# Every second low part of the weights in the first block made by GpSimd instead of VectorE

## The chip, the core and the metric

The kernel runs on one NeuronCore of a Trainium2 chip. The metric is the device time of one execution in microseconds (us), from the first to the last instruction and what lies around it. The engines are named as in the profile: PE is TensorE's matrix multiplication (PEld its weight loads), DVE is VectorE, ACT is ScalarE, POOL is GpSimd, SP the engine from which the DMAs are issued.

## What is computed

Two blocks of two layers each on 256 tokens of width 1024, all in float32. The first block is the one that the change touches: each layer is a norm, one wide input projection, a gated delta rule with 4 heads, a latent attention with 8 heads, a linear recurrence of width 512, and an output projection with a residual sum. The second block (feed-forward layers, another recurrence, two more attentions) follows it.

```python
def hybrid_layer(x, cos, sin, norm_gain, w_in, ...):
    h = rmsnorm(x, norm_gain)
    proj = h @ w_in
    (gq, gk, gv, gb, ga, gz, mq, mkv, mkr, mz, lx, lz) = jnp.split(proj, offsets, axis=-1)
    ...
    o_a = gated_delta_rule(q, k, v, g, beta)
    ...
    o_b = causal_block_attention(...).astype(dt) * jax.nn.silu(mz)
    ...
    o_c = rg_lru(u, ...).astype(dt) * jax.nn.silu(lz)
    mixed = jnp.concatenate([o_a, o_b, o_c], axis=-1)
    return x + mixed @ w_out
```

## The kernel before

Activations lie transposed, as tiles of 128 features by 256 tokens. Weights come from memory in chunks of 1 MB (`raw`, 2048 columns, 3 buffers), and every product of float32 numbers is made of three products of a shorter type (fp32r): each operand is split into a high part, which is the operand rounded to that type, and a low part, which is what the rounding left over. For the weights `wsplit` (line 680) does that: ScalarE copies the weights into `wh`, which rounds them, and VectorE subtracts `wh` from `raw` and writes `wl`. Parts of over 384 columns have buffers of their own, 3 for `wh` and 3 for `wl`, of up to 1024 columns; smaller ones lie in a pool of other tiles. A split of 1024 columns serves one unit of PE work: 8 tiles of weights, with three products each (`unit`, through `mm3`), or two, one of them twice as wide (`unit_wide`). In each unit the product with the low part of the first tile stands among the first three, so PE needs `wl` soon after `wh`.

`hybrid` (line 1314) writes down one layer of the first block: the scalars of the delta rule, the projections for the delta rule (`gdn_proj`), the latent attention (`mla_q`, `mla_kv`, `mla_pair`), the recurrence (`lru_pair`), gates, and the output projection over 16 chunks' halves (`unit_wide` and `feed`, which adds the result into `x` and prepares the next stage). The projections go through `proj`, which calls `wsplit` for 128 output features at a time. Per layer `wsplit` is called 67 times: 57 with 1024 columns, 4 with 768, 4 with 384 and 2 with 288.

None of this is the order in which the engines work. Every instruction is first noted (`Order.note`), with its dependences, and `schedule` (line 430) then plans the order of all engines together, with a duration for each from `cost` (line 378), the buffers in `SLOTS`, and a priority by place in the program. It then issues the instructions in the planned order; on the chip each engine works through its own list in order. For GpSimd `cost` books 147 + 2.11 ns for each column (line 411), for a VectorE subtraction 68 + 1.042 ns. `trace` (line 1758) writes down the whole program and calls `hybrid` for layers 0 and 1 at lines 1775 and 1799.

GpSimd has work of its own in the first block: masks, sums of squares, rope products, and powers (`pow`, on a few columns). All loads are issued by SP.

Of the kernel before, what the change touches and what calls it, by code (L numbers as in the profile page):

```python
# [9 lines left out]
F32 = mybir.dt.float32  # L10
# [3 lines left out]
ALU = mybir.AluOpType  # L14
# [275 lines left out]
class Tracer:  # L290


    def __init__(self, order, eng):
        self.order, self.eng = order, eng
# [252 lines left out]
class Kern:  # L547
    def __init__(self, ctx, tc, aps):
        self.tc, self.aps = tc, aps
        nc = self.nc = Order(tc.nc)  # L550
        self.n = 0
        self.const = ctx.enter_context(tc.tile_pool(name="const", bufs=1))
        self.pool = ctx.enter_context(tc.tile_pool(name="work", bufs=1))
        self.ps = ctx.enter_context(tc.tile_pool(name="ps", bufs=1, space=PSUM))
        self.x = self.fixed([P, 8, S], "x")
        self.prm = self.fixed([P, NPRM], "prm")
        self.cst = self.fixed([P, NCST], "cst")
        self.ident = self.c("ident")
        self.ones = self.c("ones")
        self.tri_ones = self.const.tile([P, S], F32R, tag="tri_ones", name="tri_ones")  # L560
        self.ones_r = self.tri_ones[:, P:S]
        self.mhalf = self.fixed([P, 1], "mhalf")
        self.phalf = self.fixed([P, 1], "phalf")
        self.tiny = self.fixed([P, 1], "tiny")
        nc.vector.memset(self.mhalf, -0.5)
        nc.vector.memset(self.phalf, 0.5)
        nc.vector.memset(self.tiny, 1e-34)
        self.off = {}

        self.dram = ctx.enter_context(tc.tile_pool(name="dram", bufs=1, space=DRAM))  # L570
        n = 64 * 2064
        self.tri_in = self.dram.tile([n], F32, tag="tri_in", name="tri_in")
        self.tri_out = [self.dram.tile([n], F32, tag=f"tri_out{g}", name=f"tri_out{g}") for g in range(2)]
        self.rows = self.dram.tile([12, 3, P], F32, tag="rows", name="rows")
# [105 lines left out]
    def wsplit(self, src):  # L680
        nc = self.nc
        shape = (P, src.shape[1], src.shape[2])
        n = shape[1] * shape[2]
        h = self.tile("wh" if n > 384 else "s3", shape, F32R)
        l = self.tile("wl" if n > 384 else "s3", shape, F32R)
        nc.scalar.activation(h, src, AF.Copy)
        nc.vector.tensor_tensor(l, src, h.bitcast(F32), ALU.subtract)
        return h, l

    def mm3(self, out, a, b, start, stop):  # L690
# [1058 lines left out]
def build(tc, aps, out, stop=None):  # L1749
    with ExitStack() as ctx:  # L1750
        K = Kern(ctx, tc, aps)
        trace(K, out, stop)
        K.nc.schedule()
        with tc.manual_schedule():
            K.nc.issue()


def trace(K, out, stop):
    nc, V = K.nc, K.nc.vector

    def done(tag):
        if stop == tag:
            nc.sync.dma_start(out.rearrange("p (k t) -> p k t", k=8), K.x)
            return True
        return False

    def stage(gain, fin=K.fin_x, **kw):
        st = K.new_stage(gain, **kw)
        st["fin"] = fin
        return st  # L1770
    raw = K.start()
    st = stage(K.p("norm_gain0"))
    K.first_stage(st)
    nxt = stage(K.p("norm_gain1"))
    K.hybrid(0, st, [nxt], raw)
    if done("h0"):
        return


    fg = K.fixed([P, 8], "fg")  # L1780
    V.tensor_tensor(fg, K.p("fin"), K.p("f1n0"), ALU.mult)

    def fin2(st):
        v1, ms2 = K.meansq(st["sq"]), K.meansq(st["sq2"])
        r1, v2, r2, r12 = [K.col(2) for _ in range(4)]
        K.pow(r1, v1, -0.5)
        V.tensor_scalar(v2, ms2, -1e-6, None, ALU.add)
        V.tensor_tensor(v2, v2, r1, ALU.mult)
        V.tensor_tensor(v2, v2, r1, ALU.mult)
        V.tensor_scalar(v2, v2, 1e-6, None, ALU.add)  # L1790
        K.pow(r2, v2, -0.5)
        V.tensor_tensor(r12, r2, r1, ALU.mult)
        st["rb"] = K.bcast(r12)
        r1b = K.bcast(r1)
        for k in range(8):
            V.scalar_tensor_tensor(K.x[:, k, :], K.x[:, k, :], K.p("fin", k, 1), r1b, ALU.mult, ALU.mult)
    st = nxt
    nxt = stage(fg, fin2, sq_gain=K.p("fin"))
    K.hybrid(1, st, [nxt], [K.chunk("win1", 4, 72) for _ in range(2)])
    if done("fin"):  # L1800
        return
    K.memory()
    st, nxt = nxt, stage(K.p("mix0"))
    K.ffn(st, "gu10", "dn10", [nxt])
    if done("f10"):
        return
    st, nxt = nxt, stage(K.p("f2n0"))
    K.hgrn(st, [nxt])
    if done("m0"):
        return  # L1810
    st, nxt = nxt, stage(K.p("f1n1"))
    K.ffn(st, "gu20", "dn20", [nxt])
    K.shared_kv(nxt)
    st, nxt = nxt, stage(K.p("mix1"))
    K.ffn(st, "gu11", "dn11", [nxt])
    if done("f11"):
        return
    st, nxt = nxt, stage(K.p("f2n1"))
    K.fox(st, [nxt])
    if done("m1"):  # L1820
        return
    K.ffn(nxt, "gu21", "dn21", [])
    ov = out.rearrange("p (k t) -> p k t", k=8)
    for j in range(8):
        nc.sync.dma_start(ov[:, j, :], K.x[:, j, :])
# [16 lines left out]
```

## Time and profile before

| | us |
|---|---|
| median of 3 runs | 1556.71 |
| lowest and highest | 1555.79, 1559.02 |
| the profiled execution | 1554.0 |
| its span, first to last instruction | 1552.2 |

The first block takes the first 490 us or so of the span (the feed-forward weights of the second block are first loaded at 506 us). In the rows below, a row of instructions shows the engine, the operation, the tiles as out<-in and their shapes; `s` and `col` are general tiles in SBUF, `acc` and `mix` are in PSUM, `x` is the residual, `cst` and `prm` are constants and parameters, all in SBUF. All lines are L543, the line that issues the planned order, so groups are told apart by their tiles.

### The profile page before, as it was taken

What the parts mean: (1) busy time and instruction counts of PE and PEld (TensorE: products, weight loads), DVE (VectorE), ACT (ScalarE), POOL (GpSimd) and SP (SyncE); (2) the same over time, 40 slices, a digit from 0 to 9 for tenths busy, and PEclk for the clock granted to TensorE, in tenths of its full rate; (3) what the DMA queues carried; (4) which work ended last, traced back from release to release, by engine and by line L of the source; (5) the groups of instructions that cost most, each with busy time, mean ns of one, the idle gap of its engine ahead of it and who ended that gap; (6) DMA issues with size and microseconds to landing.
All of it is one profiled execution on the core that took longest, in us unless ns stands there. A gap on an engine that the chain in (4) does not pass through costs nothing.

```text
span 1552.2 us, 27102 instructions
## 1 busy us (share of the span) xinstructions
PE 1528.0 (98%) x10216; PEld 1383.8 (89%) x10216; DVE 1209.6 (78%) x2459; ACT 892.8 (58%) x1689; POOL 324.8 (21%) x372
## 2 busy tenths in 40 slices
PE   8999999999999999999999999999999999999998
PEld 8989999998988988889997888889888889888887
DVE  8998979996998777667889777665777677877764
ACT  5458755457776666546455555555665567555542
POOL 2300002310214222202112222121222321132210
PEclk9999999999999999999999999999999999999999
DMA  8343545342545555553334555554555743355553
GB/s 285 121 121 135 167 148 186 118 150 110 166 149 178 178 190 190 190 191 128 129 137 136 190 190 176 188 180 163 191 190 181 258 138 110 136 172 184 181 188 118
DMA packets 54587, 257.58 MB, mean 166 GB/s; under 512 B 11308, under 2 KB 21688, under 8 KB 27576
## 3 DMA queue, kind: packets, MB, share of 16 engines
q1 hardware_dynamic: 54456, 255.85, 48.6%
q8 instruction: 81, 1.33, 0.4%
q14 instruction: 50, 0.41, 0.1%
HBM read 252.39 MB, written 3.43 MB: 165 GB/s over the span
## 4 chain that ended last, share of the span: by engine, by line
PE 83%; DVE 10%; issue 2%; ACT 2%; POOL 2%; DMA 1%; SPq 0%; POOLq 0%; DVEq 0%
PE acc L543 73%; PE mix L543 10%; DVE s L543 6%; DVE wl L543 2%; POOL col L543 2%; ACT s L543 1%; DVE x L543 1%; DVE col L543 1%; ACT wh L543 1%; DMA s<-tri_in 0%; POOL s L543 0%; DMA x<-in_x_dram 0%; ACT L543 0%; SPq L543 0%; POOLq L543 0%
## 5 line engine op out<-in xcount | busy, mean ns | idle before, releaser
L543 PE MATMUL acc<-s,wh 128*128 128x512 f32 (+1 forms) x4224 | 1216.9, 353 | 3.8 <-DVE x L543 2.8
L543 PE MATMUL acc<-s,wl 128*128 128x256 f32 x3360 | 951.3, 283 | 0.1
L543 PEld LDWEIGHTS acc<-s,wh 128*128 128x128 f32 x4224 | 743.3, 190 | 116.2 <-DVE s L543 2.9
L543 ACT ACTIVATE wh<-raw 128x1024 fp32r<-128x1024 f32 (+1 forms) x470 | 489.4, 1041 | 492.5 <-PE acc L543 397.0
L543 DVE TENSOR_TENSOR wl<-raw,wh 128x1024 fp32r<-128x1024 f32 (+1 forms) x470 | 569.2, 1212 | 199.7 <-ACT wh L543 195.3
L543 PEld LDWEIGHTS acc<-s,wl 128*128 128x128 f32 x3360 | 638.5, 190 | 2.0 <-DVE wl L543 0.7
L543 POOL TENSOR_TENSOR s<-s,s 128x256 f32<-128x256 f32 x251 | 220.7, 880 | 712.2 <-DVE s L543 360.7
L543 DVE TENSOR_TENSOR s<-s,s 128x256 fp32r<-128x256 f32 (+6 forms) x302 | 131.5, 446 | 36.7 <-POOL s L543 30.4
L543 PE MATMUL mix<-s,s 128*128 128x128 f32 (+5 forms) x1072 | 150.6, 280 | 5.1 <-DVE s L543 1.9
L543 ACT ACTIVATE s<-s 128x256 fp32r<-128x256 f32 (+3 forms) x311 | 135.6, 445 | 21.3 <-DVE s L543 17.7
L543 PEld LDWEIGHTS mix<-s,s 128*128 128x128 f32 (+4 forms) x1072 | 119.3, 166 | 22.8 <-DVE s L543 4.3
L543 PE MATMUL acc<-wh,s 128*128 128x256 f32 x640 | 125.5, 288 | 0.1
L543 DVE TENSOR_TENSOR s<-acc,s 128x256 f32<-128x256 f32 (+2 forms) x222 | 104.5, 471 | 10.8 <-PE acc L543 9.6
L543 PEld LDWEIGHTS acc<-wh,s 128*128 128x128 f32 x640 | 102.6, 191 | 0.9 <-ACT s L543 0.5
L543 ACT ACTIVATE s<-acc 128x256 f32<-128x256 f32 (+2 forms) x231 | 88.7, 387 | 24.5 <-PE acc L543 24.1
L543 DVE SCALAR_TENSOR_TENSOR x<-acc,x 128x256 f32<-128x256 f32 x192 | 78.3, 420 | 25.9 <-PE acc L543 23.4
L543 POOL TENSOR_TENSOR col<-col,mhalf 128x2 f32<-128x2 f32 (+2 forms) x31 | 47.0, 1519 | 220.8 <-DVE col L543 188.2
L543 PE MATMUL acc<-wl,s 128*128 128x256 f32 x320 | 91.8, 287 | 0.0
L543 ACT ACTIVATE s<-mix 128x128 f32<-128x128 f32 (+6 forms) x208 | 65.3, 328 | 43.6 <-PE mix L543 41.0
L543 DVE SCALAR_TENSOR_TENSOR s<-s,s 128x256 f32<-128x256 f32 (+2 forms) x168 | 82.4, 495 | 2.0 <-ACT s L543 1.7
L543 POOL TENSOR_TENSOR s<-s,cst 128x256 f32<-128x256 f32 x36 | 35.3, 991 | 160.3 <-DVE s L543 120.2
L543 PEld LDWEIGHTS acc<-wl,s 128*128 128x128 f32 x320 | 61.2, 191 | 0.2
(96 smaller groups left out, 772.3 us busy)
## 6 DMA issues: line engine op xcount, KB each, us to landing
raw<-in_gu_dram SPq DMA_DIRECT2D x88, 1024.0 KB, 4.9
raw<-in_win_dram SPq DMA_DIRECT2D x36, 1024.0 KB, 4.9
raw<-in_dn_dram SPq DMA_DIRECT2D x32, 1024.0 KB, 4.9
raw<-in_wo_dram SPq DMA_DIRECT2D x24, 1024.0 KB, 4.9
raw<-in_wina_dram SPq DMA_DIRECT2D x13, 1024.0 KB, 4.9
raw<-in_dn_dram SPq DMA_DIRECT2D x16, 768.0 KB, 4.2
raw<-in_winb_dram SPq DMA_DIRECT2D x7, 1024.0 KB, 4.8
raw<-in_wkv_dram SPq DMA_DIRECT2D x6, 1024.0 KB, 4.9
```

What stands on the lines that cost most here:

```text
L543: getattr(getattr(self.nc, op.eng), op.fn)(*op.args, **op.kw)
```

## The change

A counter runs over all calls of `wsplit`. Where `share` is 2, which is set for the two calls of `hybrid` alone, and a split has more than 384 columns, the subtraction of every second call (even count) is noted for GpSimd instead of VectorE. Instruction, operands and buffers stay the same. The planner sees the other engine and its cost and plans anew.

```diff
@@ -566,6 +566,7 @@
         self.off = {}
+        self.nsplit, self.share = 0, 0
@@ -684,7 +685,9 @@
         nc.scalar.activation(h, src, AF.Copy)
-        nc.vector.tensor_tensor(l, src, h.bitcast(F32), ALU.subtract)
+        self.nsplit += 1
+        eng = nc.gpsimd if n > 384 and self.share and self.nsplit % self.share == 0 else nc.vector
+        eng.tensor_tensor(l, src, h.bitcast(F32), ALU.subtract)
         return h, l
@@ -1772,7 +1775,9 @@
+    K.share = 2
     K.hybrid(0, st, [nxt], raw)
+    K.share = 0
@@ -1796,7 +1801,9 @@
+    K.share = 2
     K.hybrid(1, st, [nxt], [K.chunk("win1", 4, 72) for _ in range(2)])
+    K.share = 0
```

## Rows read from the trace of the kernel before

**Rows 1.** The page: span, and busy time, share and instructions of two engines.

```profile
span 1552.2 us, 27102 instructions
PE 1528.0 (98%) x10216; PEld 1383.8 (89%) x10216; DVE 1209.6 (78%) x2459; ACT 892.8 (58%) x1689; POOL 324.8 (21%) x372
```

**Rows 2.** Busy time by stretch: stretch, its length, then each engine's us (instructions).

```profile
35.00:91.00 56.00, 54.30 (x421) 52.02 (x420) 55.22 (x149) 26.62 (x44) 15.98 (x15) 1.00 0.41 140
...
258.00:336.00 78.00, 76.63 (x601) 74.04 (x601) 75.02 (x208) 37.51 (x65) 20.30 (x18) 1.00 0.40 137
...
410.00:456.00 46.00, 44.96 (x347) 43.13 (x346) 45.74 (x101) 37.67 (x82) 12.38 (x11) 1.00 0.53 174
...
0.00:490.00 490.00, 479.53 (x3637) 447.21 (x3638) 435.02 (x1050) 300.82 (x625) 84.21 (x99) 0.99 0.47 157
```

**Rows 3.** Chain of waits, shares by line: 35-91, 258-336, 410-456, 185-258, 120-164 us.

```profile
by line: DVE s L543 58.4%; DVE wl L543 17.2%; PE acc L543 8.6%; PE mix L543 5.9%; issue 4.8%; POOL col L543 2.9%; DVE col L543 2.4%
...
by line: DVE s L543 37.7%; PE acc L543 30.1%; DVE wl L543 11.7%; DMA s<-tri_in 8.3%; PE mix L543 4.0%; POOL col L543 3.1%; issue 2.3%; DVE col L543 2.3%; SPq L543 0.5%; DVEq L543 0.1%
...
by line: PE acc L543 34.7%; DVE s L543 21.8%; PE mix L543 17.5%; DVE wl L543 14.6%; issue 5.9%; ACT s L543 3.1%; ACT L543 2.4%; ACT wh L543 2.1%
...
by line: PE acc L543 52.6%; PE mix L543 12.5%; issue 11.5%; DVE s L543 11.0%; DVE x L543 4.7%; DVE wl L543 3.1%; POOL s L543 2.6%; ACT wh L543 1.5%; ACT s L543 1.1%; POOLq L543 0.0%
...
by line: PE acc L543 61.2%; PE mix L543 39.1%
```

**Rows 4.** Low parts (tile wl) on DVE: all to 490 us, then three stretches.

```profile
L543 DVE TENSOR_TENSOR wl<-raw,wh x122: 944/1219/1753, 13.3 to 489.4; 128x1024 fp32r<-128x1024 f32 x114, 128x768 fp32r<-128x768 f32 x8
...
35.00:91.00 56.00, 15.67 (x14) 1.00 0.41 140
...
258.00:336.00 78.00, 22.50 (x18) 1.00 0.40 137
...
410.00:456.00 46.00, 16.22 (x13) 1.00 0.53 174
```

**Rows 5.** DVE in order of time: start us, duration us, instruction.

```profile
39.99 1.22 DVE L543 TENSOR_TENSOR wl<-raw,wh 128x1024 fp32r<-128x1024 f32 x1
41.13 0.83 DVE L543 TENSOR_SCALAR s<-s,prm 128x256 f32<-128x256 f32 x1
```

**Rows 6.** POOL by form (busy us, mean ns); then POOL and DVE at 185 us.

```profile
L543 POOL TENSOR_TENSOR s<-x 128x512 f32<-128x512 f32 x2 | 2.2, 1130 | 1.1 <-DMA x<-in_x_dram 1.1
...
185.25 0.74 POOL L543 TENSOR_TENSOR s<-s,cst 128x256 f32<-128x256 f32 x1 [44.83 <-DVE s L543]
...
185.32 1.75 DVE L543 TENSOR_TENSOR wl<-raw,wh 128x1024 fp32r<-128x1024 f32 x1
```

**Rows 7.** DVE beside a POOL instruction of 512 columns, and the next one.

```profile
6.52 1.29 DVE L543 TENSOR_TENSOR s<-s,s 128x288 fp32r<-128x288 f32 x1
7.74 0.47 DVE L543 SCALAR_TENSOR_TENSOR s<-x,prm,s 128x256 fp32r<-128x256 f32 x1
```

**Rows 8.** POOL and a DVE instruction that reads PSUM, at the same time.

```profile
84.60 0.74 POOL L543 TENSOR_TENSOR s<-s,cst 128x256 f32<-128x256 f32 x1 [5.54 <-DVE s L543]
...
84.59 0.41 DVE L543 TENSOR_TENSOR s<-acc,cst 128x256 f32<-128x256 f32 x1
```

**Rows 9.** A piece of the chain (PE units); ACT's longest wait to 490 us.

```profile
164.09 20.53 PE acc L543 x171
...
ACT wh L543 <- PE acc L543: 79.9, 57, 4.0
```

**Rows 10.** POOL and DVE at 318 us, in order of time.

```profile
318.19 2.85 POOL L543 TENSOR_TENSOR s<-s,cst 128x256 f32<-128x256 f32 x1 [1.27 <-DVE s L543]
...
318.43 0.95 DVE L543 TENSOR_TENSOR wl<-raw,wh 128x768 fp32r<-128x768 f32 x1
```

**Rows 11.** The page, ACT's high parts; SP's issues of the second layer's output weights.

```profile
L543 ACT ACTIVATE wh<-raw 128x1024 fp32r<-128x1024 f32 (+1 forms) x470 | 489.4, 1041 | 492.5 <-PE acc L543 397.0
...
430.24 43.96 SPq L543 DMA_DIRECT2D raw<-in_wo_dram x8
```

## The prediction, made before the change was run

> **What bounds the kernel now.** I read the page first: the span is 1552.2 us, TensorE (PE) is busy 1528.0 us of it and VectorE (DVE) 1209.6 us [rows 1]. By that alone DVE looks like the engine with room. But the averages cover two blocks, and only the first is changed, so I took the table by stretches next, for the first 490 us [rows 2]. There DVE is busy 435.02 us of 490, and in three stretches it has nothing left: 55.22 of 56 us (35 to 91), 75.02 of 78 (258 to 336) and 45.74 of 46 (410 to 456). PE's busy time is modelled at its ends, so which of the two is late has to come from the chain of waits, taken for each stretch [rows 3]. In 35 to 91 the chain runs through DVE for 58.4 + 17.2 + 2.4 = 78% of its length, in 258 to 336 for 37.7 + 11.7 + 2.3 = 52%, in 410 to 456 for 21.8 + 14.6 = 36%. In 120 to 164 it is PE alone. So the three stretches, 180 us together, are set by DVE or by DVE and PE in turn, and the rest of the first block mostly by PE. GpSimd (POOL) is busy only 84.21 us of the 490 [rows 2].
>
> **What is moved.** wsplit (line 680) makes a high part (ScalarE, line 686) and a low part wl = raw - wh (DVE, line 687). The counter also runs over the small splits, which stay on DVE. hybrid has 67 splits for each layer; two of 288 and four of 384 columns are too small, so 61 count, 122 in both layers, as the trace also has it [rows 4]. Counting through, the even ones among them are 30 in layer 0 and 31 in layer 1: 61 subtractions move, 57 of 1024 columns and 4 of 768. In the three DVE-bound stretches stand 14 + 18 + 13 = 45 of them [rows 4], so about 22.5 move there and 38.5 elsewhere. No DMA is moved, nothing changes in the second block but what the re-planned order may shift (I allow 2 us either way).
>
> **What DVE saves.** A subtraction lasts 1.22 us, but the next DVE instruction starts 1.14 us after it (39.99 to 41.13) [rows 5]. So 1.14 us for each: 61 x 1.14 = 70 us (the four smaller ones a little less), 22.5 x 1.14 = 26 us of it where DVE sets the pace.
>
> **What POOL takes.** No POOL subtraction of 1024 columns with this output type is in the trace. Nearest rows: 256 columns with two operands take 0.74 us alone [rows 6], two instructions of 512 columns with one operand 2.2 us, so 1.1 us each [rows 6]. A line through the two, (1.1 - 0.74)/256 = 1.4 ns for each column, gives 0.74 + 768 x 0.0014 = 1.8 us. I take more, for two reads in place of one, from the next term: 2.3 us. POOL has the time: 84 + 61 x 2.3 = 225 us of 490.
>
> [...]
>
> **What POOL does to DVE.** This term decides. At 185.25 POOL starts a 0.74 us instruction; the DVE subtraction that begins at 185.32 takes 1.75 us in place of 1.22 [rows 6]: it stood still for 0.53 us, some seven tenths of POOL's instruction. It scales with size: beside the 512-column instruction, a DVE operation on 288 columns takes 1.29 us, where the next, on 256 columns, takes 0.47 [rows 7]. And it depends on where DVE reads: at 84.59 DVE reads PSUM and one SBUF operand and takes 0.41 us right beside a POOL instruction that takes its usual 0.74 [rows 8]. So POOL and the DVE instructions whose operands are all in SBUF exclude one another, for the time in which POOL reads and writes, 0.53 us for 256 columns. For 1024 columns that is 4 x 0.53 = 2.1 us, and with the 0.74 - 0.53 = 0.2 us around it the 2.3 us above. Bounds for the stall of each moved subtraction: 0 (DVE is idle or reads PSUM all the while) to 2.1 us. In the dense stretches DVE always has a next instruction, and at most one or two of its PSUM readers (0.41 us [rows 8]) come before one that must wait; I take 2.1 - 0.35 = 1.75 us. Net on DVE: between -1.14 and +0.98 us for each moved subtraction, taken +0.61 us. The work leaves DVE, and more than its time comes back as standing still.
>
> **The sum.** Three dense stretches: 22.5 x 0.61 = +13.7 us of DVE time. DVE's idle time there is 0.78 + 2.98 + 0.26 = 4.0 us, so +9.7 us comes out at the end. Elsewhere: 38.5 x 0.61 = +23.5 us, beside 310 - 259.0 = 51 us of DVE idle time; the cover is that PE is the one that is late (the chain of 120 to 164, PE only [rows 3]). If that cover were gone the whole 23.5 us would be paid. Some is: the stretch 185 to 258 has DVE in 11.0 + 4.7 + 3.1 = 19% of its chain [rows 3], and a wait of 2 us in an attention chain is not always hidden. I take +3 us, of 0 to 12. In all +13 us on the profiled execution: 1554.0 becomes 1567. That execution is 2.7 us below the median of the three runs, 1556.7, so the forecast is 1556.7 + 13 = 1569.7 us. With stalls of 1.4 us the dense stretches give 22.5 x 0.26 - 4 = +2 us; with 2.1 us, 22.5 x 0.98 - 4 = +18 us and up to 12 us more elsewhere. Its own range is 1559 to 1587.
>
> **What is queued behind.** POOL works in order. Behind a moved subtraction stand the masks, rope sums and powers, the shortest of them 0.74 us [rows 6]. The planner (cost, line 411) books 2.3 us for it and knows nothing of the exclusion (its lists for DVE and POOL are independent), so it will fill the time taken from DVE with other DVE work and send it into the stalls. The raw buffer is freed later by up to 1.2 us plus the wait for DVE, which delays the next 1 MB load; three raw buffers cover that, as each serves two units of PE work of about 24 x 0.12 = 2.9 us (171 matmuls in 20.53 us [rows 9]).
>
> **Rivals.**
> Gain: the stalls fall into DVE's idle and PSUM time, and the relief counts. For it: 11% of DVE's time in the first block is idle. Against: not where DVE is late. What can be won is bounded by PE: the three stretches hold 421 + 601 + 347 = 1369 matmuls [rows 2], which at 0.12 us [rows 9] need at least 164 of the 180 us. So 16 us at the most; I price this at -8 us, 1549 us. [...]
>
> Late low parts: POOL starves, and PE waits for wl. At 318.19 POOL needed 2.85 us for a 0.74 us instruction, while DVE went through a subtraction of 768 columns in 0.95 us [rows 10], the shortest time there is for one (944 ns [rows 4]). DVE went first there, and more than once. The point from which it decides is the lead of the three wh and wl buffers: the buffer comes free when PE ends a unit (ScalarE waits 79.9 us for that [rows 9]), and two units, 5.8 us, later the part must be there; ScalarE takes 1.0 us [rows 11], POOL 2.3 us, which leaves some 2.3 us for waiting (semaphores take part of it). One delay as at 318 uses it up. If every moved subtraction came 0.5 us late, 61 x 0.5 = 30 us would come on top of the 13: 1600 us.
>
> [...]
>
> Nothing to measure: relief and stalls cancel (a stall of about 1.3 us), or PE's lateness covers both: 1554 to 1559 us.
>
> **How the numbers follow.** 0.2% of the time, 3 us, is about what a measurement of this kernel can tell from no change. Forecast 0.58, late parts 0.13, nothing to measure 0.13, gain 0.16. So slower 0.71, same 0.13, faster 0.16. The range 1550 to 1592 leaves out half of the gain and most of the late case.
>
> **What would show it.** In the profile after: about 61 wl rows on POOL, near 2.3 us where alone and up to 3.5 us where they wait; DVE rows of SBUF operations that are 1.5 to 2.1 us longer than their usual time, while rows that read PSUM stay; DVE's busy time in the first block at 450 us or more, although 61 instructions are gone; the chain of the dense stretches still on DVE; the loads of the second layer's output weights start later than 430.24 us [rows 11], and from there on the time is as before. Wrong would be: DVE busy near 435 - 70 = 365 us, or a POOL instruction of 1024 columns that lets DVE through in between; then the time falls. Many PE waits for wl would be the late case.

## The result, and the profile after

| | before | after |
|---|---|---|
| median of 4 runs each, on one chip | 1557.44 us | 1639.33 us |
| lowest and highest | 1555.79, 1559.02 | 1628.38, 1643.16 |
| span of the profiled execution | 1552.2 us | 1637.2 us |

The change makes the kernel slower: the ratio is 1.0514, with an interval of 1.0484 to 1.0545. That is +82 us where +13 was forecast: the direction was right, the size was not, and 1639 lies far outside the range of 1550 to 1592.

The page of the kernel after: the span, the busy time of each engine, then the slices of PE, DVE and of PE's granted clock (tenths, 40 slices).

```profile
span 1637.2 us, 27169 instructions
PE 1566.3 (96%) x10216; PEld 1412.5 (86%) x10216; DVE 1221.9 (75%) x2398; ACT 890.9 (54%) x1689; POOL 470.3 (29%) x433
PE   8789989978998999999999999999999999999999
DVE  8884886889399667776788977767677677887764
PEclk9897999989799999999999999999999999999999
```

Against [rows 1], the 85.0 us that the span has gained divide in two. PE does the same 10216 matmuls in 1566.3 us in place of 1528.0, so it is busy 38.3 us longer; and it stands idle 1637.2 - 1566.3 = 70.9 us in place of 1552.2 - 1528.0 = 24.2, which is 46.7 us more. DVE has 61 instructions less and is busy 12.3 us more.

All of it lies in the first block. The next table ends at the first load of the feed-forward weights, 506 us before and 592 us after; behind it both kernels take 1045 to 1046 us more. Columns: stretch, its length, busy us (instructions) of PE, PEld, DVE, ACT and POOL, granted clock of PE, DMA share, GB/s. The kernel before:

```profile
0.00:506.00 506.00, 494.75 (x3747) 461.45 (x3748) 447.69 (x1080) 311.24 (x644) 94.69 (x110) 0.99 0.47 156
```

The kernel after: the whole block, then 120 to 164, 410 to 456 and 482 to 538 us.

```profile
0.00:592.00 592.00, 532.90 (x3745) 490.80 (x3746) 462.12 (x1019) 309.71 (x643) 238.41 (x171) 0.92 0.39 133
...
120.00:164.00 44.00, 43.70 (x336) 37.07 (x335) 19.72 (x53) 22.24 (x73) 3.43 (x2) 0.77 0.26 85
...
410.00:456.00 46.00, 46.00 (x348) 39.40 (x349) 21.96 (x49) 28.20 (x87) 10.56 (x7) 0.74 0.22 82
...
482.00:538.00 56.00, 48.43 (x346) 45.83 (x346) 53.16 (x99) 36.36 (x80) 27.14 (x18) 0.94 0.42 143
```

PE's idle time in the block grows from 506 - 494.75 = 11 to 592 - 532.90 = 59 us, 48 us more, and its busy time for the same matmuls but two from 494.75 to 532.90, 38 us more. The two make the 86 us of the block. The longer busy time goes with the granted clock, which falls from 0.99 to 0.92: (1 - 0.92) x 592 - 0.01 x 506 = 42 us by these rounded means.

The work of a stretch now stands later, so the same interval of the two traces is not the same work. By the count of matmuls, what stands in 410 to 456 us of the kernel after is what the kernel before does in 347 to 386 us, outside the dense stretches:

```profile
347.00:386.00 39.00, 38.64 (x351) 33.56 (x350) 24.43 (x59) 28.94 (x93) 2.48 (x3) 0.96 0.30 109
```

PE sets this work in both kernels, and nearly the same matmuls take 46 us at a mean clock of 0.74 in place of 39 at 0.96: this is what the clock costs. The dense work of 410 to 456 in [rows 2] has moved to 482 to 538 us, and there DVE is busy for 53.16 of 56 us. The chain of waits says the same, here for 13 to 120, 410 to 456 and 482 to 538 us of the kernel after:

```profile
by line: DVE s L543 37.9%; PE acc L543 24.0%; PE mix L543 13.7%; DVE wl L543 8.6%; DVE col L543 8.0%; issue 4.0%; ACT wh L543 2.0%; ACT s L543 1.0%; POOL col L543 0.9%; POOLq L543 0.0%; ACTq L543 0.0%
...
by line: PE mix L543 55.7%; PE acc L543 19.2%; DVE s L543 17.4%; issue 3.6%; DVE wl L543 2.5%; ACT s L543 2.2%; ACT L543 0.6%; DVE col L543 0.1%
...
by line: DVE s L543 53.6%; PE acc L543 13.8%; DVE wl L543 13.7%; PE mix L543 9.7%; issue 6.2%; ACT s L543 3.2%; DVEq L543 0.1%
```

Next, who makes PE wait. The waits of the kernel after (engine and tile, what ended the wait, us in total, times, longest):

```profile
PE mix L543 <- DVE s L543: 39.4, 18, 6.1
...
PE acc L543 <- POOL wl L543: 0.7, 1, 0.7
```

and of the kernel before:

```profile
PE mix L543 <- DVE s L543: 3.0, 7, 1.0
```

PE hardly ever waits for a low part made by POOL. It waits for DVE's small results (`s`), 39.4 us in place of 3.0, which feed the short chains of products in `mix`. One of these waits, in the kernel after, shows all the parts of the story. POOL, then DVE, then PE, in order of time (start us, us, instruction, in brackets the idle time before it and its releaser):

```profile
44.86 2.37 POOL L543 TENSOR_TENSOR wl<-raw,wh 128x1024 fp32r<-128x1024 f32 x1
47.19 1.45 POOL L543 TENSOR_TENSOR s<-s,cst 128x256 f32<-128x256 f32 x2
...
45.04 2.21 DVE L543 TENSOR_SCALAR col<-col 128x2 f32<-128x2 f32 x1
47.17 0.15 DVE L543 SCALAR_TENSOR_TENSOR col<-col,col 128x8 f32<-128x8 f32 x1
47.24 1.54 DVE L543 TENSOR_SCALAR s<-s,prm 128x256 f32<-128x256 f32 x2
48.71 2.44 DVE L543 SCALAR_TENSOR_TENSOR s<-s,prm,s 128x255 f32<-128x255 f32 x6
...
45.97 0.28 PE L543 MATMUL acc<-s,wl 128*128 128x256 f32 x1
52.33 2.08 PE L543 MATMUL mix<-s 128*128 128x256 f32 x4 [6.08 <-DVE s L543]
```

POOL begins a moved subtraction at 44.86. The DVE instruction that comes up at 45.04 has two columns and takes 2.21 us: it goes on only when POOL is done. POOL's next two small instructions then stretch DVE's pair at 47.24 to 1.54 us. PE has nothing to do from 46.25 and waits 6.08 us for a result that stands further down in DVE's list. After that the granted clock is at half, 0.50, for the next 10 us (rows under e5).

### The profile page after: what moved, and what is told of

It reads as the page before. It is cut to its first block, busy times and chain, and to the rows that moved or that the text cites. A ratio compares the mean times of both kernels' runs of the same rounds, so it can differ in the third digit from the quotient of the medians.

```text
span 1637.2 us, 27169 instructions
## 1 busy us (share of the span) xinstructions
PE 1566.3 (96%) x10216; PEld 1412.5 (86%) x10216; DVE 1221.9 (75%) x2398; ACT 890.9 (54%) x1689; POOL 470.3 (29%) x433
## 4 chain that ended last, share of the span: by engine, by line
PE 76%; DVE 15%; issue 3%; ACT 3%; POOL 2%; DMA 1%; SPq 0%; POOLq 0%; DVEq 0%; ACTq 0%
PE acc L543 65%; PE mix L543 11%; DVE s L543 11%; ACT s L543 2%; DVE wl L543 2%; POOL col L543 1%; DVE col L543 1%; DVE x L543 1%; ACT wh L543 1%; POOL s L543 1%; DMA x<-in_x_dram 0%; DMA s<-tri_in 0%; POOL wl L543 0%; SPq L543 0%; ACT L543 0%
## 5 line engine op out<-in xcount | busy, mean ns | idle before, releaser
L543 DVE TENSOR_TENSOR wl<-raw,wh 128x1024 fp32r<-128x1024 f32 (+1 forms) x409 | 500.2, 1223 | 200.9 <-ACT wh L543 197.9
L543 POOL TENSOR_TENSOR wl<-raw,wh 128x1024 fp32r<-128x1024 f32 (+1 forms) x61 | 150.0, 2458 | 245.7 <-ACT wh L543 207.3
L543 PE MATMUL mix<-s,s 128*128 128x128 f32 (+5 forms) x1072 | 165.5, 304 | 15.3 <-DVE s L543 13.2
L543 DVE TENSOR_TENSOR s<-s,s 128x256 f32<-128x256 f32 (+6 forms) x302 | 141.1, 478 | 35.2 <-POOL s L543 30.4
L543 PEld LDWEIGHTS mix<-s,s 128*128 128x128 f32 (+4 forms) x1072 | 131.5, 184 | 36.0 <-DVE s L543 13.7
L543 DVE SCALAR_TENSOR_TENSOR s<-s,s 128x256 f32<-128x256 f32 (+2 forms) x168 | 96.1, 580 | 10.1 <-ACT s L543 9.7
L543 ACT ACTIVATE s<-acc 128x256 f32<-128x256 f32 (+2 forms) x231 | 88.5, 386 | 26.4 <-PE acc L543 25.7
L543 ACT ACTIVATE s<-mix 32x64 f32<-32x64 f32 (+6 forms) x208 | 64.7, 325 | 68.5 <-PE mix L543 65.9
L543 POOL TENSOR_TENSOR col<-col,mhalf 128x2 f32<-128x2 f32 (+2 forms) x31 | 46.7, 1506 | 159.1 <-DVE col L543 126.4
L543 PE MATMUL mix<-cst,s 128*128 128x128 f32 (+2 forms) x338 | 59.6, 274 | 11.8 <-DVE s L543 6.8
```

The source lines that it names most:

```text
L543: getattr(getattr(self.nc, op.eng), op.fn)(*op.args, **op.kw)
```

## The experiments

I summed for each kernel, up to the first load of the feed-forward weights, what DVE's instructions took above the median of their form in the kernel before beside no POOL work (from 0.2 us up; "holds"), and the time at half clock. "Idle" is PE's idle time there, from its first matmul on; "mix" is PE's time waiting in `mix` for DVE's `s`; the change of the median is against the runs of the kernel before on the same chip.

| kernel | median us | change us | idle | half clock | DVE holds (over 1 us) | mix |
|---|---|---|---|---|---|---|
| before | 1557.44 | | 10.1 | 10.2 | 24.6 (0) | 3.0 |
| after | 1639.33 | +82 | 57.9 | 99.0 | 103.1 (39) | 39.4 |
| e1 new order, DVE subtracts | 1587.57 | +30 | 32.4 | 54.6 | 25.7 (0) | 23.9 |
| e2 old order, POOL subtracts | 1609.98 | +52 | 40.8 | 51.2 | 103.2 (39) | 19.9 |
| e3 output projection alone | 1569.49 | +12 | 16.0 | 30.7 | 37.0 (6) | 6.2 |
| e4 pieces of 256 columns | 1624.56 | +67 | 47.3 | 71.7 | 79.3 (0) | 33.5 |
| e5 PE kept busy | 1624.85 | +69 | 35.3 | 64.9 | 103.2 (39) | 18.0 |
| e6 planner knows of the hold | 1614.57 | +59 | 45.0 | 51.1 | 75.4 (27) | 2.0 |
| e7 POOL reads beside | 1649.57 | +94 | 67.7 | 81.9 | 96.2 (0) | 30.9 |
| e8 POOL writes beside | 1590.23 | +35 | 24.7 | 54.6 | 22.0 (0) | 11.9 |
| e9 no elementwise work on POOL | 1559.88 | +3 | 12.2 | 13.7 | 3.1 (0) | 1.3 |
| e10 new order, 61 left out | 1566.26 | +9 | 15.4 | 27.3 | 37.8 (3) | 8.3 |
| e11 old order, 61 left out | 1554.80 | -2 | 9.4 | 23.9 | 33.7 (3) | 3.2 |
| e12 old order, two writes | 1567.56 | +11 | 14.3 | 20.5 | 43.1 (3) | 7.5 |

Between e2, e3, e8 or e12 and the kernel before, 3 to 8 us of the spans' difference lie behind the first feed-forward load; I did not follow these up. Only e2, e6, e7 and e9 landed inside a range that was expected of them, and e9 in both of its two; the others fell between or beside their ranges, so they are read here by what their traces show.

### e1 and e2: the order and the engine, each alone

The change does two things: the planner makes another order for all engines, and the subtraction runs elsewhere. e1 takes the new order and lets DVE do the work; e2 takes the old order and lets POOL do it.

```diff
 # both: at the place of issue
-            getattr(getattr(self.nc, op.eng), op.fn)(*op.args, **op.kw)
+            getattr(getattr(self.nc, getattr(op, "lab", op.eng)), op.fn)(*op.args, **op.kw)
 # e1, on the kernel after, in wsplit
+        if eng is nc.gpsimd:
+            nc.ops[-1].lab = "vector"
 # e2, on the kernel before, in wsplit, share set as in the change
+        if n > 384 and self.share and self.nsplit % self.share == 0:
+            nc.ops[-1].lab = "gpsimd"
```

> The order of all engines is the one planned for the changed kernel (1639 us), but the 61 subtractions are carried out by DVE at the same places. Theory A (POOL's subtraction stops DVE for 2.1 us, PE waits for DVE, and its clock falls to half after the waits): no hold of POOL is left and DVE has its 61 x 1.14 = 70 us back, in an order that did not reckon with them; 1552 to 1572 us, half-clock time of the first block back near 10 us (96 in the changed kernel). Theory B (the new order, written for a DVE that was thought relieved, is itself the slow part): 1600 us or more. Theory C (low parts come late because POOL takes 2.4 us for one): as A, since DVE makes them in 1.2 us.

> The order planned for the kernel before (1557 us), with the same 61 subtractions carried out by POOL at the same places. Theory A: the stalls are there as in the changed kernel; 1600 to 1640 us, DVE rows of SBUF operations 2.1 us longer beside POOL's, half-clock time 50 us or more. Theory B: the order is the good one; 1560 to 1580 us. Theory C: PE's waits that end with a low part of POOL sum to 20 us or more (they are 1.9 us in the changed kernel).

Measured: e1 1.0201 (1.0161 to 1.0240), +30 us; e2 1.033 (1.0295 to 1.0366), +52 us. The sum is the +82 us of the change. Where DVE does all the work again (e1), its holds are those of before, 25.7 us, and PE still waits 23.9 us in `mix`: the new order counts on 70 us of DVE time that DVE does not have here (e10, where DVE has it, bears this out). In e2 the holds are exactly those of after, 103.2 us in 39 long ones, without any change of order. So neither part alone is the cause, and the bigger one is POOL's work itself.

### e3: only the output projection

Here 16 subtractions move, all in the output projections, where PE was to be late and to cover DVE. The planner plans anew for them, so the order changes too.

```diff
-    K.share = 2          # around both calls of hybrid
+        self.share = 2   # around the two loops of the output projection
```

> Only the 16 subtractions of the output projections move to POOL (8 in each layer); the other 45 stay on DVE. Theory A: there PE is late and DVE mostly reads PSUM, so the stalls are covered; 1554 to 1561 us, half-clock time as before. If each moved subtraction cost the same, 16/61 of 82 us = +21: 1578 us. Theory C: 16 parts late by 0.5 us, +8: 1565 us.

Measured: 1.0074 (1.0052 to 1.0095), +12 us. That is 0.7 us for each moved subtraction, near the 52 / 61 = 0.85 of e2. The prediction had put 38.5 of them, outside the dense stretches, at 3 us together. The long holds are 6 of 16 here; what else costs can be seen at the end of the block. POOL and PE in e3:

```profile
498.82 2.41 POOL L543 TENSOR_TENSOR wl<-raw,wh 128x1024 fp32r<-128x1024 f32 x1
501.19 4.18 POOL L543 TENSOR_TENSOR s<-s,s 128x256 f32<-128x256 f32 x4
...
510.12 1.40 POOL L543 TENSOR_TENSOR s<-s,s 128x256 f32<-128x256 f32 x2
...
510.89 1.01 PE L543 MATMUL mix<-cst,s 128*128 128x1 f32 x4 [2.79 <-POOL s L543]
```

The sums of squares for the next norm (`s<-s,s`) stand behind the last subtraction in POOL's list, and PE's first product of that norm waits 2.79 us for them; the longest such wait in the kernel before is 0.78 us. PE has no other work at that seam to cover the wait. Part of the +12 us is the clock (30.7 us at half clock, 10.2 before).

### e4: shorter instructions

Each of the 61 is cut into pieces of 256 columns.

```diff
+            if getattr(op, "lab", None) == "pieces":   # l, a, h, f: wl, raw, wh, subtract
+                for i in range(0, k * m, 256):
+                    self.nc.gpsimd.tensor_tensor(l[c], a[c], h[c], f)   # c: columns i to i + 256
```

> Order and engines as in the changed kernel, but each of POOL's 61 subtractions is issued as pieces of 256 columns, 4 of 0.74 us for 1024 columns (3 for 768). The time for which POOL holds DVE off is the same in sum (about 61 x 2.1 = 128 us), one hold is 0.53 us. If the length of one hold decides (a DVE operation gets in between two pieces, so none waits for more than 0.53 us): 1570 to 1605 us. If the sum of the holds decides, or POOL's next piece goes ahead of DVE: 1630 to 1655 us. DVE's longest rows tell it directly: +0.5 us against +2.1 us.

Measured: 1.0425 (1.0390 to 1.0459), +67 us. The longest hold falls from 2.23 to 0.84 us, but 165 of them still add up to 79.3 us, and the median gains 15 us. So shorter holds, which are also 24 us less in sum, give back 15 of the 82 us; the rest of the harm stays with short ones.

### e5: does PE's clock fall because PE waits?

In the kernel after's order, products that nobody uses are put ahead of those matmuls for which PE had waited, as many as fit 0.85 of the wait. They go to the area that the next product overwrites. Not every wait could be filled: that of 5.1 us that begins at 110 us was left.

```diff
+                wait = WAITS.get(seen, 0)       # ns, this matmul's wait in the trace of after
+                    for _ in range(int(0.85 * wait / (120 if cols == 256 else 220))):
+                        mm(flat, self.fill[0][:, :P], self.fill[0], start=True, stop=True)
```

> As the changed kernel, but in front of 24 or so of the matmuls that waited longest in its trace (0.4 to 6.1 us, 50 us together) PE is given 217 products of constants, whose results are overwritten, to fill about 85% of the wait. They do nothing for DVE or POOL. In the changed kernel PE was idle 48 us longer in the first block than before, and did 79 us more of its work at half clock, which makes 40 us. Theory A (the waits themselves take away the clock): half-clock time falls from 99 us towards 20, the idle time turns into filler, and the time falls to 1595 to 1620 us. If the clock falls for another reason: half-clock time stays at 80 us or more and the time stays at 1635 to 1665 us.

Measured: 1.0441 (1.0408 to 1.0474), +69 us, so 14.5 us less than after by the medians (11 by the ratios), with more PE work and the same holds (103.2 us). The trace by stretches, columns as above. The kernel after:

```profile
46.00:50.00 4.00, 0.25 (x3) 0.04 (x1) 4.00 (x8) 0.00 (x0) 2.64 (x3) 0.99 0.47 197
50.00:60.00 10.00, 7.67 (x24) 6.60 (x25) 6.08 (x29) 2.19 (x4) 0.72 (x1) 0.50 0.29 109
...
111.00:115.00 4.00, 0.00 (x0) 0.00 (x0) 4.00 (x4) 0.18 (x1) 2.78 (x1) 0.98 0.00 0
...
118.40:131.90 13.50, 13.50 (x109) 12.48 (x108) 9.86 (x29) 6.49 (x16) 2.41 (x1) 1.00 0.49 139
131.90:152.40 20.50, 20.50 (x128) 16.65 (x127) 7.79 (x22) 6.20 (x23) 0.00 (x0) 0.50 0.22 88
```

e5:

```profile
46.00:50.00 4.00, 4.00 (x36) 4.00 (x35) 4.00 (x5) 0.00 (x0) 4.00 (x4) 1.00 0.75 262
50.00:60.00 10.00, 10.00 (x76) 9.69 (x76) 8.70 (x37) 3.13 (x5) 1.61 (x2) 1.00 0.33 117
...
107.00:111.00 4.00, 0.00 (x0) 0.00 (x0) 4.00 (x4) 0.25 (x1) 2.86 (x1) 0.97 0.00 0
...
127.00:149.00 22.00, 21.98 (x137) 17.78 (x137) 8.10 (x22) 6.68 (x26) 0.00 (x0) 0.53 0.24 92
```

With PE idle in 46 to 50 the clock is 0.50 in 50 to 60; with PE busy there it is 1.00. The pieces at half clock near 77, 333, 360 and 395 us are gone in e5 as well, where the waits ahead of them were filled; one of 3.4 us at 39 has come up, and the one at the start is 6.8 us longer. Time at half clock falls from 99.0 to 64.9 us; counting half of PE's busy time in it as lost, that is 44.7 us in the kernel after and 30.7 in e5, 14 us, about what the medians have. So at least this part is shown: the waits that could be filled cost PE their own length, and then more, because it comes out of them at half clock. The longest piece, 20.5 us from 132 on, stays in e5, behind the wait that could not be filled; but between the two PE of the kernel after is busy for 13.50 of 13.50 us at full clock, so what brings that piece on stays open.

It is not the only one. Of the twelve pieces of the kernel after, nine, 54.6 us together, begin in a wait of PE of about 0.9 us or more or within 1.3 us of its end. The other three, at 132, 412 and 436 us, 44.4 us together, do not, and PE is busy all through them. Here is the middle one, whose nearest wait was of 0.87 us and ended 2.7 us ahead of it:

```profile
411.80:428.80 17.00, 17.00 (x112) 12.99 (x111) 6.97 (x19) 6.17 (x23) 1.82 (x1) 0.50 0.22 80
```

They hold 22.2 of the 44.7 us that were counted as lost. The kernel before has such a piece too, of 3.4 us at 371 us, in the work that the kernel after does at 410 to 456. Why it is so much longer in the kernel after no run here shows.

### e6: tell the planner

In `schedule` a POOL subtraction of 768 columns or more now starts only when DVE is free, and DVE is booked as busy while it lasts.

```diff
+            hold = e == "gpsimd" and op.fn == "tensor_tensor" and _free(op.args[0]) >= 768
+            if hold:
+                t = max(t, free["vector"])
 ...
+            if hold:
+                free["vector"] = t + d
```

> The same 61 subtractions on POOL, but the planner is told of the exclusion: while it places one of them, DVE is booked as occupied for the same 2.3 us. Two parts add up so far: the old order with POOL's subtractions costs 52 us, the new order with DVE's subtractions 30 us, both together 82. If the 30 us are the price of an order written in ignorance of the stalls, they go, and some of the 52 as well, as PE's work is laid around the stalls: 1575 to 1610 us. If the stalls cost what they cost wherever they stand: 1610 to 1640 us.

Measured: 1.0394 (1.0337 to 1.0451), +59 us, just inside what was expected if the stalls cost the same wherever they stand. Some 20 us of the 82 come back (23 by the medians, 19 by the ratios), and PE's waits in `mix` for DVE go from 39.4 to 2.0 us, but waits in `acc` for it come up (17.8 us) and 27 long holds stay; why they stay was not looked into. That is less than the 29 us that the new order adds to e2, and the plan is a third order whose parts were not taken apart.

### e7 and e8: what POOL's instruction does to DVE

The old order, and DVE does all subtractions. At each of the 61 places POOL gets a one-column instruction that waits for `wh`, and then either three that read constants (e7) or six that only write zeros (e8), 341 columns each.

```diff
+                g.tensor_tensor(junk[:, 0:1], h[:, 0, 0:1], h[:, 0, 0:1], ALU.mult)
 # e7
+                for _ in range(3):
+                    g.tensor_tensor(junk, cst[:, 0:341], cst[:, 512:853], ALU.subtract)
 # e8
+                for _ in range(6):
+                    g.memset(junk, 0.0)
```

> The kernel before with its order, all subtractions on DVE. At the 61 places POOL is given work of no use beside it: 3 subtractions of 341 columns of constants (about 0.9 us each, 2.7 us together) behind a one-column instruction that waits for the high part. DVE is relieved of nothing. If reading by POOL is what stops DVE: 61 x 3 x 0.7 = 128 us of holds come on top of a DVE that is busy 89%, so the time is above the 52 us of the old order with POOL's subtractions: 1630 to 1690 us. If POOL's subtractions hurt only by coming late: 1557 to 1570 us.

> As the run before, but POOL's work of no use is 6 memsets of 341 columns (about 0.4 us each, 2.4 us together), which write and read nothing. If POOL's reads of SBUF are what stops DVE, DVE rows keep their usual lengths and the time stays near that of before: 1555 to 1570 us, what there is coming from POOL's own instructions, which stand 2.4 us behind. If any work of POOL in SBUF stops DVE: as the run with reads, 1630 us or more.

Measured: e7 1.0614 (1.0573 to 1.0655), +94 us; e8 1.0224 (1.0183 to 1.0265), +35 us. The added work at each place is 3 x 1.22 = 3.7 us in e7 and 6 x 0.39 = 2.4 us in e8, so the two do not differ by the reading alone, and DVE's rows have to decide. e7: its first block, POOL's added instructions to 598 us, and POOL and DVE in order of time.

```profile
0.00:598.00 598.00, 529.08 (x3741) 486.75 (x3742) 518.91 (x1080) 310.35 (x642) 352.51 (x354) 0.93 0.40 132
...
L548 POOL TENSOR_TENSOR junk<-cst 128x341 f32<-128x341 f32 x183 | 223.4, 1221 | 14.4
...
67.53 3.20 POOL L548 TENSOR_TENSOR junk<-cst 128x341 f32<-128x341 f32 x3
...
68.16 1.80 DVE L543 SCALAR_TENSOR_TENSOR s<-s,s 128x256 f32<-128x256 f32 x2
```

e8, the same views:

```profile
0.00:538.00 538.00, 512.15 (x3737) 476.54 (x3738) 446.88 (x1080) 310.24 (x641) 282.56 (x537) 0.95 0.44 147
...
L548 POOL MEMSET junk<- 128x341 f32 x366 | 143.9, 393 | 21.2
...
66.48 2.65 POOL L548 MEMSET junk<- 128x341 f32 x6
...
67.40 2.44 DVE L543 SCALAR_TENSOR_TENSOR s<-s,prm,s 128x255 f32<-128x255 f32 x6
69.76 1.22 DVE L543 TENSOR_TENSOR wl<-raw,wh 128x1024 fp32r<-128x1024 f32 x1
70.90 0.75 DVE L543 SCALAR_TENSOR_TENSOR s<-s,s 128x256 f32<-128x256 f32 x2
```

In e8 DVE's six instructions take 2.44 us right beside POOL's writes, and 446.88 us in all, as before (447.69). In e7 a pair that takes 0.75 us alone takes 1.80, and DVE is busy for 518.91 us. So it is POOL's reading that stops DVE's instructions here: DVE is busy 72 us longer in e7 than in e8, with 96.2 us of holds. But e8 costs 35 us with no more holds of DVE than the kernel before has (22.0 and 24.6 us): POOL's own results come later (DVE waits 12.7 us for its `s`, in six waits of up to 3.1 us), and the one-column instruction keeps `wh` a little longer, for which ScalarE waits 12.4 us. How the 35 us divide between these two was not measured.

Writing is not free of holds, though. The short writes of e8 hold DVE ten times, for 2.2 us together; writes of 1024 columns, as in e12 below, hold it 30 times beside no other POOL work, for 17.0 us together. Of these 30 rows 28 are TENSOR_SCALAR, COPY or RECIPROCAL, which read one tile, some with a column of scalars beside it. A pair of writes of e12, and one DVE form beside them and behind them:

```profile
332.02 1.99 POOL L545 MEMSET wl<- 128x1024 f32 x2
...
333.04 1.11 DVE L547 TENSOR_SCALAR s<-s,cst 128x256 f32<-128x256 f32 x1
...
334.14 0.34 DVE L547 TENSOR_SCALAR s<-s,cst 128x256 f32<-128x256 f32 x1
```

### e9: is there something to gain in the other direction?

If holds cost so much, those of the kernel before (24.6 us, all under 0.84) should too. Here POOL's elementwise work of the first block goes to DVE, except the powers; the planner plans anew.

```diff
+        if eng == "gpsimd" and self.onv and fn == "tensor_tensor" and args[3] != ALU.pow:
+            eng = "vector"
```

> The other way round: all 61 subtractions are on DVE as in the kernel before, and the sums, products and masks that POOL had in the first block (some 58 of 256 columns) go to DVE too; POOL keeps the powers. Each held DVE off for up to 0.53 us (24.6 us of DVE's time in the first block of the kernel before) and took 0.74 us or more itself; on DVE one takes about 0.35 to 0.45 us. If the exclusion is what matters, DVE's load is the same and the results come earlier: 1545 to 1562 us. If DVE's load alone matters, as before: 1555 to 1575 us.

Measured: 1.0023 (1.0004 to 1.0042), +3 us. The holds fall to 3.1 us and nothing is gained; DVE is busy as long as before (446.67 us). What the holds took, DVE now spends on the work itself, so moving this work to DVE does not pay; what short holds cost by themselves this run does not say.

### e10 to e12: the work left out

To price the relief by itself, the 61 subtractions are left out, and with them the low part of these weights; POOL writes zeros into `wl` in their place, so that buffers and waits stay: once in the new order (e10) and the old one (e11), twice in the old order (e12).

```diff
+            if getattr(op, "lab", None) == "part":
+                for _ in range(1):                  # e12: range(2)
+                    self.nc.gpsimd.memset(op.args[0].bitcast(F32), 0.0)
+                continue
```

> The order of the changed kernel, with the 61 subtractions left out: POOL fills those low parts with zeros (one memset, about 1.1 us, reads nothing), so part of the product is missing. DVE has the relief that the planner counted on and is stopped by nothing new. If the order is good for what it was planned for, and the 30 us of the run with DVE's subtractions in this order came from 70 us of DVE work that it had not booked: 1535 to 1560 us. If the order is worse in itself: 1575 us or more.

> The same in the order of the kernel before: DVE is relieved of 61 subtractions (70 us), POOL does a memset of 1.1 us for each, the low parts are zeros. What the relief is worth at most with PE's order as it was: the three stretches where DVE is late give 10 to 16 us: 1540 to 1550 us. If POOL's own results come later behind the memsets and that outweighs it: 1557 to 1575 us.

> As the run before, with two memsets for each low part (about 2.2 us, nearly as long as POOL's subtraction of 2.4 us, but without reading). Against the old order with POOL's subtractions (+52 us) only the stalls of DVE are taken away. If the stalls are the price: 1540 to 1562 us. If POOL's own results, queued behind 2.4 us each time, are the price (the memsets beside a full DVE cost 35 us): 1575 to 1600 us.

Measured: e10 1.0063 (1.0023 to 1.0103), e11 0.9978 (0.9960 to 0.9997), e12 1.0069 (1.0050 to 1.0087). e11's first block and its writes on POOL:

```profile
0.00:508.00 508.00, 497.40 (x3746) 464.02 (x3747) 388.28 (x1019) 310.21 (x643) 145.41 (x171) 0.98 0.46 155
...
L545 POOL MEMSET wl<- 128x1024 f32 (+1 forms) x61 | 57.3, 941 | 216.5 <-PE acc L547 206.5 <-issue 10.0
```

DVE is busy 388.28 us in place of 447.69, 59 us less, and the kernel gains 2 us (0.5 to 6 by the interval). That is the whole worth of the relief in this order, with POOL's queue taxed by 0.94 us at each place and no hold from a read, but with 9 us more of holds than before. With 1.9 us at each place (e12) the same kernel is 13 us slower than e11, and its holds are another 9 us more. The new order, with DVE really relieved (e10), is 9 us slower than before, not faster: it was no better an order to begin with. But in that order the relief is worth 21 us (e1 - e10), since it was planned for it. In these three kernels PE multiplies zeros in place of the low parts; whether that alone changes its time was not tested.

### What the parts cost

In the old order, by the medians: relief -2 us (e11); a second write at each place, for POOL's longer queue and the 9 us of holds that it adds, +13 (e12 - e11); POOL's subtraction in place of the two writes, with 60 us of holds more, +42 (e2 - e12, 1609.98 - 1567.56). These are the steps from the kernel before to e2, so that they add up to its +52 is no test of them. The split between queue and holds is only as good as 1.9 us of writing stands for 2.4 us of reading.

The new order then adds 29 (after - e2, 1639.33 - 1609.98), and e1 shows it alone as 30. By itself, with the relief that it counts on, it costs 9 (e10); the rest comes where DVE does not have that time, in e1 because it does the work, in the kernel after, it seems, because it is held.

Of the 82 us, 38 are PE's longer busy time at the lower clock. They come on top of its waits where the pieces at half clock stand behind these, which e5 shows for about 14 us; the pieces without a wait, 22 us by the same count, stay open.

No version that computes everything beats the kernel before.

## Why the prediction was right or wrong, step by step

**What moved and what POOL takes: right.** 61 low parts are on POOL, 57 of 1024 columns and 4 of 768. All on POOL to 592 us in the kernel after (count, busy us, mean ns, idle time before them):

```profile
L543 POOL TENSOR_TENSOR wl<-raw,wh 128x1024 fp32r<-128x1024 f32 x57 | 142.0, 2491 | 222.1 <-ACT wh L543 193.7 <-DVE s L543 18.1 <-PE acc L543 4.8
...
L543 POOL TENSOR_TENSOR wl<-raw,wh 128x768 fp32r<-128x768 f32 x4 | 8.0, 1988 | 23.5 <-ACT wh L543 13.6 <-PE acc L543 10.0
```

The forecast was 2.3 us where alone and up to 3.5 where it waits; most take 2.40, the mean is 2.49. The line through [rows 6] alone gave 1.8 us; the 2.3 came from scaling the hold of the same rows.

**The hold: right in size.** 2.1 us was taken for 1024 columns, scaled from the 0.53 us of [rows 6]; the longest is 2.23 us. DVE's readers of PSUM pass, as [rows 8] had it. POOL and DVE of the kernel after, in order of time:

```profile
260.00 2.41 POOL L543 TENSOR_TENSOR wl<-raw,wh 128x1024 fp32r<-128x1024 f32 x1 [8.81 <-ACT wh L543]
...
258.94 0.88 DVE L543 SCALAR_TENSOR_TENSOR x<-acc,x 128x256 f32<-128x256 f32 x2
261.71 0.88 DVE L543 SCALAR_TENSOR_TENSOR x<-acc,x 128x256 f32<-128x256 f32 x2 [1.89 <-PE acc L543]
```

The pair at 261.71 begins beside POOL's subtraction and takes the same 0.88 us as the pair before it. The mean hold for a moved subtraction, (103.1 - 24.6) / 61 = 1.29 us, is below the 1.75 taken. The mechanism is narrower than "reads and writes": POOL's writes alone hold few of DVE's instructions (ten for 2.2 us in e8, 30 for 17.0 us in e12), its reads hold many (DVE's holds are 96.2 us in e7, 24.6 before). DVE's busy time of the block, 462 us, is above the 450 named, but the 61 x 0.61 = 37 us that it was to gain net are 14.

**The sum: wrong, and this is the step that failed.** The mechanism behind it was right; what it did with the parts was not. It netted DVE's relief against its holds (1.75 - 1.14 = 0.61 us each) and then took DVE's idle time off the rest. That treats DVE as a store of time in which a microsecond won here pays for one lost there. By its own rule, with the hold as it was measured, 61 x (1.29 - 1.14) = 9 us of DVE time would have come out, less the cover: next to no change. So it was in part luck that the forecast had the right direction: it took the hold longer than it is. The runs show that the two do not net: in the old order 59 us of relief are worth 2 us (e11), while the 103.2 - 43.1 = 60 us of holds that e2 has more than e12 cost 42. A hold is paid at its place by whoever waits for the next result, as PE does for 6.08 us at 46.25; time saved elsewhere seems to bring forward results that nobody waits for yet, which no run here shows by itself.

**The cover outside the dense stretches: wrong.** It was PE's lateness, worth 3 us for 38.5 subtractions. e3 moves 16, of which 14 stand outside those stretches, and costs 12 us. The chain of 120 to 164 in [rows 3], PE only, does say that PE is late there; it does not hold for the seams between stages, such as that of e3, where PE waits 2.79 us for POOL.

**What is queued behind: named, and priced at nothing.** "POOL works in order", and the planner "will fill the time taken from DVE with other DVE work and send it into the stalls": both sentences are right, and neither has a term in the sum. In the trace of after POOL's subtraction of 44.86 us lasts 2.37 us, and the products behind it begin at 47.19, as it ends. The runs have about +13 us for the first (e12 - e11, with 9 us of holds by writes in it) and +29 us for the second (after - e2).

**The clock: not thought of.** The sum has no term for PE's granted clock, though the profile of before has it in every row of stretches, at 1.00 in the dense ones [rows 2]. It was taken as given. PE's busy time is 38 us longer by it, about half of that in pieces that begin at a wait of PE.

**The rivals.** Late low parts, 1600 us: false as a mechanism, since PE waits 0.7 us for `wl` from POOL (and PEld 1.2). Three buffers are lead enough. Little of the lead goes in the step from ScalarE to POOL, for which the prediction names semaphores: in the kernel after a copy ends at 259.93 us, and the subtraction on POOL that waits for it begins at 260.00, 0.07 us later. Its time is nearer to the result than the forecast's, for the wrong reason. Gain, with a ceiling of 16 us: the relief is worth 2 us where no read holds DVE (e11).

**What would show it.** Holds of 1.5 to 2.1 us on SBUF operations and none on PSUM readers: yes. The output weights of the second layer are loaded later, and from there on the time is as before: yes, 507.75 in place of 430.24 us [rows 11], 77.5 of the 85 us. The chain of the dense stretches still on DVE: yes. In 13 to 120 us DVE has 37.9 + 8.6 + 8.0 = 55% of it, and the third dense stretch, now at 482 to 538, has 53.6 + 13.7 = 67% in place of 36.

## What to carry to other kernels

Where engines work lists in order, do not net an engine's relief against its delays: price the relief by leaving the work out, price each delay at the consumer that waits for it, since the two can differ widely (here 2 us for 59 of relief in the order that was not planned for it, 42 for 60 of holds). Before work goes to an engine whose instructions were seen to hold up the loaded one, ask which of them read SBUF (DVE's holds are 96.2 us beside reads in e7, 22.0 beside short writes in e8), and what of its own stands behind the new, long ones. And where PE is at full clock, a wait of PE can cost more than its length: look for time at a lower clock behind it (here some 14 us, e5), and compare the same work in two traces, not the same interval.

## What the runs showed of the hardware that was not expected

- PE's granted clock was at half for 99.0 us of the first block in place of 10.2, in pieces of 3.4 to 20.5 us. Pieces of 54.6 us together begin at or just behind a wait of PE; three, of 44.4 us, come with PE busy throughout. Unused products in such a wait kept the clock at 1.00 (e5, 50 to 60 us).
- The hold does not depend on the size of the DVE instruction that it meets: one of two columns takes 2.21 us at 45.04, which is what POOL's instruction still had to run; the small one after it, of eight, takes 0.15.
- POOL writing zeros in short instructions left DVE's busy time as it was (446.88 us with 366 more of 341 columns, 447.69 without), POOL reading did not (518.91 us with 183). Writes of 1024 columns held DVE's instructions that read one tile, for up to 0.79 us each (e12).
